# Value projections of two mixers in one set of 512-column products, and where they stand

## The chip, the cores and the metric

The program runs on one core of one Trainium2 chip. The metric is the device time of one execution in microseconds (us). Five engines matter: TensorE (products; its weight loads are listed apart as PEld), VectorE (DVE), ScalarE (ACT), GpSimd (POOL) and SyncE (SP), whose queue issues all DMAs. Each engine runs its own instructions in a fixed order and waits on semaphores for the others.

## What is computed

Two transformer blocks, each of two layers, on one sequence of 512 tokens with 1024 features. The change is in the first block. A layer of it is a gated feed-forward, a stage of four mixers, and another feed-forward. All mixers read one projection of the normalised input `z = rmsnorm(x) @ w_in`:

```python
(aq, ak, av, iq, ik, iw, bq, bk, bv, bg, br, cu, dcq, dckv, dkpe) = split(z)
y_a = dsa_mixer(aq, ak, av, iq, ik, iw, ...)   # attention on the 128 best keys of an index
y_b = gla_mixer(bq, bk, bv, bg, br, ...)       # gated linear attention
y_c = conv_mixer(cu, ...)                      # gate, causal convolution of 31 taps, norm, silu
y_d = mla_mixer(dcq, dckv, dkpe, ...)          # attention on latents, with rotated parts
x = x + concat(y_a, y_b, y_c, y_d) @ w_out
```

`av` and `bv`, the values of mixers A and B, are 256 columns each; they are plain projections of `x`. The values of mixer D come from the 128 latents of `dckv` and have 256 columns too.

## The kernel before

Activations lie with features on the 128 partitions and the 512 tokens in columns; 128 x 512 float32 numbers fill one of the eight PSUM banks. To keep float32 accuracy every operand is split into a high part and a rest (`wh`, `wl` of the weights, `xnh`, `xnl` of the input), and each product is three TensorE instructions (`mm3`, lines 196 to 198: high by high, high by rest, rest by high).

**Weights.** `Model.fill` takes them in the order that `order` lists: a DMA of up to 512 KB into one of three `raw` buffers, a ScalarE copy that rounds to `wh` (line 181), a VectorE subtraction that gives `wl` (line 182). Three pairs of `wh`/`wl` exist. `weights` keeps up to two loads ahead of the one that is asked for.

**The order of work.** The kernel is written in a framework that plans the instructions when the program is built: the order in which the code issues them is a priority, and the planner, with modelled times of its own, puts on each engine's queue the first by priority that it takes to be ready, and a later one where an earlier would wait. The chip then runs each queue in that fixed order, also where the real times are others.

**The mixers' stage** (`Mixers.run`) issues: the misc and latent projections, mixer A's index scores, `d_heads` (mixer D's queries, keys and values; its norms need spread products `sp`, line 592, and rotation products `rot`, line 1052), and `c_prep` (the four `cu` projections of 24 products each; its result is written to DRAM as `hp_d`). Then, interleaved by generators: eight steps of mixer D's attention (`d_attend`); with each, one of sixteen rounds of mixer A's top-k on VectorE (`a_topk`) and three steps of a side chain: `c_conv`, `a_values`, `a_heads`, `c_out`. After that come the rest of the top-k, `b_heads` (projections `bq`, `bk`, each taken from PSUM by VectorE, line 523), `b_values`, `b_gates` (`br0`, `br1`), `a_bias` (tables of mixer A's position bias, loaded into tiles that D's attention frees), and mixer A's attention `a_attend`, whose bias products are line 772, with the rest of mixer B beside it.

**The convolution** takes two halves of 128 channels. For each half it loads taps (line 954) and shifted rows of `hp_d` (line 957, four DMAs) into a tile of tag `gq`, of which there is one, then issues 32 products of 32 rows by 512 columns in plain float32 (line 962; each shows as two records) and a copy from PSUM. Between loads and products stands one `yield`.

**The values.** `values` (line 556 on) makes 128 tokens by 256 columns at a time: 24 products with the tokens' input as weights and 256 columns of `w_v` moving, then a ScalarE eviction (line 565); four blocks for A, four for B. The results of A lie two blocks to a tile in R2 and R3, of B in R0 and R1; `d_heads` uses R0 to R4 before. Projections and values share two PSUM banks (tag `mm`). In `d_heads` the four blocks of D's values (name `uv`) each take a bank of `mm` for 256 columns and an eviction (line 1035).

Of the kernel before, what the change touches and what calls it, by code (L numbers as in the profile page):

```python
# [10 lines left out]
FR = mybir.dt.float32r  # L11
# [3 lines left out]
AF = mybir.ActivationFunctionType  # L15
# [5 lines left out]
KD = D // 128  # L21
# [11 lines left out]
def pack_values(w):  # L33

    return np.ascontiguousarray(w.reshape(2, 4, 128, 256).transpose(0, 2, 1, 3))


def cols(v):
# [23 lines left out]
class Model:  # L62
# [107 lines left out]
    def fill(self, n):  # L170

        nc = self.nc
        while len(self.loaded) < n and self.todo:
            src = self.todo.popleft()
            flat = src if len(src.shape) == 2 else src.rearrange("p a b -> p (a b)") if len(src.shape) == 3 \
                else src.rearrange("p a b c d -> p (a b c d)") if len(src.shape) == 5 else src.rearrange("p a b c -> p (a b c)")
            cols = flat.shape[1]
            raw = self.wp.tile([128, cols], F32, name="raw", tag="raw", bufs=NRAW)
            nc.sync.dma_start(raw, flat)
            h, l = (self.wp.tile([128, cols], FR, name=n, tag=n, bufs=3) for n in ("wh", "wl"))  # L180
            nc.scalar.activation(h, raw, AF.Copy)  # L181
            nc.vector.tensor_tensor(l, raw, h.bitcast(F32), op=ALU.subtract)  # L182
            self.loaded.append((src, (h, l)))
# [161 lines left out]
LEAD = 16  # L345
LOOKAHEAD = 2
NRAW = 3
PARTS = ((0, 8), (8, 7), (15, 7))
HALVES = (slice(0, S // 2), slice(S // 2, S))

# [94 lines left out]
def host_pack_mixers(I, P, vadd):  # L445
    for l in range(2):
        w = I["w_in"][l]
        misc = np.zeros((D, 128), w.dtype)
        for n, c, r in (("ik", 32, 0), ("dkpe", 32, 32), ("iw", 8, 64), ("bg", 16, 96)):
            misc[:, r:r + c] = w[:, IN_OFF[n]:IN_OFF[n] + c]  # L450
        t = [misc]
        for n in IN_TILES[1:]:
            b, j = (n[:-1], int(n[-1])) if n[-1].isdigit() else (n, 0)
            t.append(w[:, IN_OFF[b] + 128 * j:IN_OFF[b] + 128 * (j + 1)])
        P[f"w_in{l}"] = pack_T(np.concatenate(t, axis=1))
        P[f"w_v{l}"] = np.stack([pack_values(w[:, IN_OFF[n]:IN_OFF[n] + 256]) for n in ("av", "bv")])
        uq = I["d_uq"][l].reshape(256, 4, 96)
        uq = np.concatenate([uq[:, :, :64].reshape(256, 256), uq[:, :, 64:].reshape(256, 128)], axis=1)
        P[f"d_uq{l}"] = np.ascontiguousarray(pack_T(uq).transpose(1, 0, 2, 3))
        ukv = I["d_ukv"][l].reshape(128, 4, 128)  # L460
        P[f"d_ukv{l}"] = np.ascontiguousarray(
            np.concatenate([ukv[:, :, :64].reshape(128, 256), ukv[:, :, 64:].reshape(128, 256)], axis=1))
        g = np.zeros((128, 128), np.float32)
        g[96:112] = I["b_gate_up"][l]
        P[f"b_up{l}"] = g

        wo = I["w_out"][l]
        P[f"w_out{l}"] = pack_T(np.concatenate([wo[512:768], wo[768:1024], wo[256:512], wo[0:256]], axis=0))
        two = lambda a: np.tile(a.reshape(1, -1), (2, 1)).reshape(-1, 1)
        vadd(f"a_q_norm{l}", two(I["a_q_norm"][l]))  # L470
        vadd(f"a_k_norm{l}", two(I["a_k_norm"][l]))
        vadd(f"b_gate_bias{l}", cols(I["b_gate_bias"][l]))
        vadd(f"b_out_norm{l}", two(I["b_out_norm"][l]))
        w = I["c_dw_w"][l][:, 0, :]
        taps = np.zeros((2, 4, 32, 4, 8, 32), w.dtype)
        c = np.arange(32)
        for k in range(31):
            taps[:, k % 4, c, :, k // 4, c] = w[k].reshape(2, 4, 32).transpose(2, 0, 1)
        P[f"c_taps{l}"] = taps.reshape(2, 128, 4, 8, 32)
        vadd(f"c_b{l}", cols(I["c_dw_b"][l]))  # L480
        vadd(f"c_norm{l}", cols(I["c_norm"][l]))
        vadd(f"d_qa_norm{l}", cols(I["d_qa_norm"][l]))
        vadd(f"d_kva_norm{l}", cols(I["d_kva_norm"][l]))
        for n in ("d_q_norm", "d_k_norm"):
            a = I[n][l]
            vadd(f"{n}_n{l}", two(a[:64]))
            vadd(f"{n}_p{l}", np.tile(a[64:].reshape(1, -1), (4, 1)).reshape(-1, 1))
    P["rel_bias"] = I["rel_bias"]
    for n, c in constants().items():
        P["c_" + n] = c  # L490


class Phase:
# [61 lines left out]
    def values(self, w, out):  # L555
# [3 lines left out]
        for t in range(4):  # L559
# [4 lines left out]
                M.mm3(o, (M.xn[k][0][:, r], M.xn[k][1][:, r]), (ws[k // 4][0][:, s], ws[k // 4][1][:, s]), k == 0, k == KD - 1)  # L564
            nc.scalar.activation(out(t), o, AF.Copy, scale=self.rn[:, t:t + 1])


    def gather_squares(self, out, tiles):

# [63 lines left out]
class Mixers(Phase):  # L633


    def order(self):

        ap, l = self.ap, self.l
        p = lambda *ns: [ap[f"w_in{l}"][IN_TILES.index(n)] for n in ns]
        v = lambda i: [ap[f"w_v{l}"][i, c] for c in range(2)]  # L640
        return p("misc", "dcq0", "dcq1", "dckv", "iq0", "iq1") + [ap[f"d_uq{l}"], ap[f"d_ukv{l}"]] + \
            p("cu2", "cu0", "cu3", "cu1") + v(0) + p("aq0", "aq1", "ak0", "ak1", "bq", "bk") + v(1) + p("br0", "br1") + \
            [ap[f"w_out{l}"][m, :, 4 * i:4 * i + 4] for i in range(2) for m in range(KD)]

    def proj(self, name):
# [131 lines left out]
                yield  # L777


    def b_values(self):  # L780
        two = [self.z(f"vB{i}", f"R{i}") for i in range(2)]
        self.vB = [two[t // 2][:, 256 * (t % 2):256 * (t % 2) + 256] for t in range(4)]
        self.values(self.ap[f"w_v{self.l}"][1], lambda t: self.vB[t])

    def a_values(self):
        two = [self.z(f"vA{i}", f"R{2 + i}") for i in range(2)]
        self.vA = [two[t // 2][:, 256 * (t % 2):256 * (t % 2) + 256] for t in range(4)]
        self.values(self.ap[f"w_v{self.l}"][0], lambda t: self.vA[t])

    def b_heads(self):  # L790
        self.bq = self.take(self.proj("bq"), "bq", "Q0", scale=32 ** -0.5)
# [210 lines left out]
    def d_heads(self):  # L1002
# [22 lines left out]
        raw = [raw[0], raw[1], raw[3], raw[4], raw[2], kpr]  # L1025
        self.dv = []
        ch, cl = self.ckv[0]
        for t in range(4):
            o = M.psum_mm("uv")[:, :256]
            r = slice(t * 128, (t + 1) * 128)  # L1030
            M.mm3(o, (ch[:, r], cl[:, r]), (ukv[0][:, 256:512], ukv[1][:, 256:512]), True, True)
            if t % 2 == 0:
                dv = self.z(f"dv{t // 2}", f"dv{t // 2}")
            v = dv[:, 256 * (t % 2):256 * (t % 2) + 256]
            nc.scalar.activation(v, o, AF.Copy)
            self.dv.append(v)
        g = M.psum("gD")
        self.gather_squares(g, [(t, [(i, i // 2 * 2)] if i < 4 else [(2 * i - 8, 2 * i - 5), (2 * i - 7, 2 * i - 4)])
                                for i, t in enumerate(raw)])
# [60 lines left out]
    def run(self, last_tile):  # L1100
        with ExitStack() as st:
# [6 lines left out]
            def chain(*fs):  # L1108
                for f in fs:
                    g = f()  # L1110
                    if g is not None:
                        yield from g
                    yield
# [7 lines left out]
            self.d_heads()  # L1121
            self.c_prep()
            topk = self.a_topk()
            side = chain(self.c_conv, self.a_values, self.a_heads, self.c_out)
            for _ in self.d_attend():
                step(topk)
                step(side, n=3)
# [1 line left out]
                for _ in g:  # L1129
                    pass  # L1130
            self.b_heads()
            self.b_values()
            self.b_gates()
            self.a_bias()
            self.yC = [self.split_y(t) for t in self.cacc]
# [802 lines left out]
```

## Time and profile before

| what | before |
|---|---|
| device time, median of 3 runs | 3290.86 us (3290.36 to 3291.94) |
| the profiled execution | 3292.49 us, its span 3290.7 us |
| TensorE busy | 3200.9 us (97%) |
| VectorE busy | 1732.0 us (53%) |
| ScalarE busy | 1319.8 us (40%) |
| mean granted TensorE clock | 0.991 |
| mixers' stage, first layer | about 378 to 700 us |
| mixers' stage, second layer | about 1411 to 1730 us |

A profile is one execution. A record has a start, a duration and, in brackets, the idle time of its engine before it and what ended that. Products overlap in TensorE's pipeline, so the cost of one is read from the distance between starts, not from its duration. The granted clock is the share of full TensorE speed in a stretch; a value between the two levels is a mean over them.

### The profile page before, as it was taken

To read this page: it belongs to the slowest core of one execution; us is meant where nothing else is said; L and a number is where in the kernel's file an instruction comes from. 1 tells how busy PE (TensorE), PEld (TensorE's weight loads), DVE (VectorE), ACT (ScalarE), POOL (GpSimd) and SP (SyncE) were. 2 spreads that over 40 slices of the span, in tenths; PEclk is the share of its full clock that TensorE was granted. 3 is DMA by queue.
4 is the path that set the end of the run, shared out by engine and by line. 5 is a ranking of instruction groups with operands and counts; after the bars stand their busy time and mean duration, and the time that the engine had idled before them with its cause. 6 is when DMAs were issued, how large, how long until landed. Compare 5 with 4: busy or idle time off the path is not lost.

```text
span 3290.7 us, 38872 instructions
## 1 busy us (share of the span) xinstructions
PE 3200.9 (97%) x15174; PEld 2566.7 (78%) x15178; DVE 1732.0 (53%) x2767; ACT 1319.8 (40%) x2041; POOL 187.2 (6%) x184
## 2 busy tenths in 40 slices
PE   8999999999999999999999999998999999989998
PEld 6888856788888888875778888876788887778887
DVE  5443468664433444357774443687554428664433
ACT  4232346743323332243763322355533227643322
POOL 1000100010000000010010000000200011010000
PEclk9999999999999999999999999999999999999999
DMA  4333341033333332343113333322233332323332
GB/s 158 111 97 97 108 128 61 26 107 100 97 94 100 96 96 93 100 126 98 49 62 96 96 93 100 113 79 58 93 96 96 93 100 71 102 71 96 97 95 79
DMA packets 114473, 306.65 MB, mean 93 GB/s; under 512 B 21840, under 2 KB 35056, under 8 KB 114288
## 3 DMA queue, kind: packets, MB, share of 16 engines
q1 hardware_dynamic: 114288, 304.16, 29.9%
q8 instruction: 119, 1.95, 0.2%
q14 instruction: 66, 0.54, 0.0%
HBM read 292.18 MB, written 10.09 MB: 92 GB/s over the span
## 4 chain that ended last, share of the span: by engine, by line
PE 86%; DVE 6%; ACT 4%; DMA 3%; issue 1%; SPq 0%; POOL 0%; DVEq 0%; ACTq 0%; POOLq 0%
PE gu L196 14%; PE gu L197 14%; PE gu L198 14%; PE o L197 8%; PE o L198 8%; PE o L196 8%; DMA conv<-hp_d 1%; PE conv L962 1%; PE wo L197 1%; PE wo L196 1%; PE wo L198 1%; PE lgD L1080 1%; PE v L196 1%; DVE wl L182 0%; PE v L197 0%
## 5 line engine op out<-in xcount | busy, mean ns | idle before, releaser
L181 ACT ACTIVATE wh<-raw 128x1024 fp32r<-128x1024 f32 (+2 forms) x550 | 550.3, 1001 | 1492.9 <-PE gu L197 843.0
L182 DVE TENSOR_TENSOR wl<-raw,wh 128x1024 fp32r<-128x1024 f32 (+2 forms) x550 | 633.0, 1151 | 547.3 <-ACT wh L181 542.7
L196 PE MATMUL o<-hid,wh 128*128 128x512 f32 (+1 forms) x1100 | 419.2, 381 | 0.0
L197 PE MATMUL o<-hid,wh 128*128 128x512 f32 (+1 forms) x1100 | 418.9, 381 | 0.0
L198 PE MATMUL o<-hid,wl 128*128 128x512 f32 (+1 forms) x1100 | 418.5, 380 | 0.0
L315 DVE SCALAR_TENSOR_TENSOR us<-gu,rstd 128x512 f32<-128x512 f32 x132 | 91.2, 691 | 400.7 <-PE gu L198 400.7
L196 PEld LDWEIGHTS o<-hid,wh 128*128 128x128 f32 x1100 | 206.8, 188 | 39.9
L197 PEld LDWEIGHTS o<-hid,wh 128*128 128x128 f32 x1100 | 206.8, 188 | 39.8
L198 PEld LDWEIGHTS o<-hid,wl 128*128 128x128 f32 x1100 | 206.8, 188 | 39.1
L313 DVE SCALAR_TENSOR_TENSOR gs<-gu,rstd 128x512 f32<-128x512 f32 x132 | 91.3, 692 | 259.3 <-PE gu L198 258.5
L272 POOL TENSOR_TENSOR sqacc<-sqacc,sq 128x512 f32<-128x512 f32 x70 | 104.2, 1488 | 369.4 <-ACT sq L267 367.4
L318 ACT ACTIVATE hid<-gs 128x512 fp32r<-128x512 f32 x132 | 83.5, 632 | 93.1 <-DVE gs L316 93.1
L196 PE MATMUL gu<-xn0h,wh 128*128 128x512 f32 x258 | 103.3, 400 | 0.0
L197 PE MATMUL gu<-xn6l,wh 128*128 128x512 f32 x258 | 100.6, 390 | 1.9 <-DVE xn6l L261 1.9
L197 PE MATMUL gu<-xn0l,wh 128*128 128x512 f32 x258 | 100.9, 391 | 0.0
L198 PE MATMUL gu<-xn0h,wl 128*128 128x512 f32 x258 | 100.9, 391 | 0.0
L198 PE MATMUL gu<-xn1h,wl 128*128 128x512 f32 x258 | 100.9, 391 | 0.0
L197 PE MATMUL gu<-xn1l,wh 128*128 128x512 f32 x258 | 100.9, 391 | 0.0
L197 PE MATMUL gu<-xn2l,wh 128*128 128x512 f32 x258 | 100.9, 391 | 0.0
L196 PE MATMUL gu<-xn1h,wh 128*128 128x512 f32 x258 | 100.9, 391 | 0.0
L196 PE MATMUL gu<-xn2h,wh 128*128 128x512 f32 x258 | 100.8, 391 | 0.0
L198 PE MATMUL gu<-xn2h,wl 128*128 128x512 f32 x258 | 100.7, 390 | 0.0
(1386 smaller groups left out, 7069.9 us busy)
## 6 DMA issues: line engine op xcount, KB each, us to landing
raw<-in_ffn_gu SPq DMA_DIRECT2D x176, 512.0 KB
raw<-in_f_gu SPq DMA_DIRECT2D x88, 512.0 KB
raw<-in_ffn_d SPq DMA_DIRECT2D x64, 448.0 KB
raw<-in_w_in SPq DMA_DIRECT2D x36, 512.0 KB
raw<-in_ffn_d SPq DMA_DIRECT2D x32, 512.0 KB
raw<-in_f_d SPq DMA_DIRECT2D x32, 448.0 KB
raw<-in_w_out SPq DMA_DIRECT2D x32, 256.0 KB
raw<-in_f_d SPq DMA_DIRECT2D x16, 512.0 KB
```

The source lines that it names most:

```text
L181: nc.scalar.activation(h, raw, AF.Copy)
L182: nc.vector.tensor_tensor(l, raw, h.bitcast(F32), op=ALU.subtract)
L196: t.matmul(out, lhsT=wh, rhs=xh, start=first, stop=False)
L197: t.matmul(out, lhsT=wh, rhs=xl, start=False, stop=False)
L198: t.matmul(out, lhsT=wl, rhs=xh, start=False, stop=last)
L272: nc.gpsimd.tensor_tensor(self.sq_acc, self.sq_acc, sq, op=ALU.add)
L313: nc.vector.scalar_tensor_tensor(gs, g, -1.0, self.nrstd, op0=ALU.mult, op1=ALU.mult)
L315: nc.vector.scalar_tensor_tensor(us, u, -1.0, self.nrstd, op0=ALU.mult, op1=ALU.mult)
L318: nc.scalar.activation(h, gs, AF.Copy)
L962: nc.tensor.matmul(p[32 * g:32 * g + 32], lhsT=cw[:, g, k], rhs=st[:, g, 4 * k:4 * k + S], start=(k == 0), stop=(k == 7))
L1080: nc.tensor.matmul(lg[:, :C], lhsT=self.dq[h][:, q], rhs=self.dk[h][:, :C], start=True, stop=False)
```

## The change

Both values are made in one set: the weights of `av` and `bv` stand side by side, so that each block of 128 tokens needs 24 products of 512 columns, held in four weight buffers of 512 KB. The set is issued by the side chain between the first convolution half's loads and its products, a block to a step; the second half's products come after mixer A's four projections. `b_values` goes. A fourth pair of weight buffers is made (three `raw` buffers stay), and a scratch area for DMA descriptors is halved. D's values are made two blocks to a bank, with one eviction for both.

```diff
-            h, l = (self.wp.tile([128, cols], FR, name=n, tag=n, bufs=3) for n in ("wh", "wl"))
+            h, l = (self.wp.tile([128, cols], FR, name=n, tag=n, bufs=NW2) for n in ("wh", "wl"))
...
+NW2 = 4
...
+    def values_wide(self, w, out):
+
+        M, nc = self.M, self.nc
+        ws = [M.weights(w[c]) for c in range(4)]
+        for t in range(4):
+            r = slice(t * 128, (t + 1) * 128)
+            o = M.psum_mm("v")
+            for k in range(KD):
+                s = slice((k % 2) * 512, (k % 2) * 512 + 512)
+                M.mm3(o, (M.xn[k][0][:, r], M.xn[k][1][:, r]), (ws[k // 2][0][:, s], ws[k // 2][1][:, s]), k == 0, k == KD - 1)
+            nc.scalar.activation(out(t), o, AF.Copy, scale=self.rn[:, t:t + 1])
+            yield
...
-            p("cu2", "cu0", "cu3", "cu1") + v(0) + p("aq0", "aq1", "ak0", "ak1", "bq", "bk") + v(1) + p("br0", "br1") + \
+            p("cu2", "cu0", "cu3", "cu1") + v + p("aq0", "aq1", "ak0", "ak1", "bq", "bk", "br0", "br1") + \
...
+    def ab_values(self):
+
+        v = [self.z(f"vAB{t}", f"R{t}") for t in range(4)]
+        self.vA = [t[:, :256] for t in v]
+        self.vB = [t[:, 256:] for t in v]
+        yield from self.values_wide(self.ap[f"w_v{self.l}"], lambda t: v[t])
...
-        for t in range(4):
-            o = M.psum_mm("uv")[:, :256]
...
+        for i in range(2):
+            o = M.psum_mm("uv")
+            dv = self.z(f"dv{i}", f"dv{i}")
+            for t in range(2):
+                r = slice((2 * i + t) * 128, (2 * i + t + 1) * 128)
+                c = slice(256 * t, 256 * t + 256)
+                M.mm3(o[:, c], (ch[:, r], cl[:, r]), (ukv[0][:, 256:512], ukv[1][:, 256:512]), True, True)
+                self.dv.append(dv[:, c])
+            nc.scalar.activation(dv, o, AF.Copy)
...
-            side = chain(self.c_conv, self.a_values, self.a_heads, self.c_out)
+            conv = self.c_conv()
+            part = lambda: next(conv)
+            side = chain(part, self.ab_values, part, part, self.a_heads, part, self.c_out)
...
             self.b_heads()
-            self.b_values()
             self.b_gates()
...
-    nc = bacc.Bacc("TRN2", target_bir_lowering=False, num_devices=1, dynamic_dma_scratch_size=2048)
+    nc = bacc.Bacc("TRN2", target_bir_lowering=False, num_devices=1, dynamic_dma_scratch_size=1024)
```

## Rows read from the trace of the kernel before

**Rows 1.** The page, part 1: busy us, share of the span, instructions, by engine.

```profile
PE 3200.9 (97%) x15174; PEld 2566.7 (78%) x15178; DVE 1732.0 (53%) x2767; ACT 1319.8 (40%) x2041; POOL 187.2 (6%) x184
```

**Rows 2.** Stretch, length, busy us (PE, PEld, DVE, ACT, POOL), granted clock, DMA share, GB/s.

```profile
460.00:482.00 22.00, 18.63 (x86) 5.71 (x85) 13.40 (x23) 2.88 (x4) 0.00 (x0) 0.84 0.32 100
482.00:507.00 25.00, 22.16 (x159) 12.72 (x158) 20.18 (x57) 6.10 (x22) 0.20 (x1) 1.00 0.26 79
507.00:565.00 58.00, 58.00 (x289) 40.87 (x287) 52.85 (x132) 38.36 (x72) 2.48 (x4) 1.00 0.17 55
565.00:592.00 27.00, 26.36 (x188) 23.42 (x186) 12.92 (x18) 18.20 (x31) 0.53 (x1) 1.00 0.26 89
592.00:655.00 63.00, 59.33 (x359) 42.01 (x361) 44.76 (x119) 48.30 (x133) 0.00 (x0) 1.00 0.06 17
1494.00:1515.00 21.00, 17.76 (x83) 5.28 (x82) 12.69 (x22) 2.55 (x4) 0.00 (x0) 0.84 0.33 103
```

**Rows 3.** Waits of TensorE, whole kernel: us in total, times, longest us.

```profile
PE conv L962 <- DMA conv<-hp_d: 12.8, 10, 2.8
...
PE gb L196 <- ACT wh L181: 1.4, 3, 0.9
```

**Rows 4.** Timeline of TensorE: start, us, instruction, idle before and its releaser.

```profile
460.17 0.39 PE L198 MATMUL cu<-xn7h,wl 128*128 128x512 f32 x1
...
465.96 1.92 PE L962 MATMUL conv<-conv 128*32 128x512 f32 x2 [2.79 <-DMA conv<-hp_d]
...
478.39 1.12 PE L1052 MATMUL rot<-kpr,c_rot 128*128 128x512 f32 x2
...
480.14 1.06 PE L962 MATMUL conv<-conv 128*32 128x512 f32 x6
...
481.13 0.38 PE L197 MATMUL v<-wl,xn1h 128*128 128x256 f32 x1
```

**Rows 5.** Timeline of TensorE, 490 to 507 us.

```profile
490.38 0.28 PE L196 MATMUL v<-wh,xn6h 128*128 128x256 f32 x1
...
501.36 5.35 PE L962 MATMUL conv<-conv 128*32 128x512 f32 x46
...
506.64 0.39 PE L196 MATMUL v<-wh,xn1h 128*128 128x256 f32 x1
```

**Rows 6.** Timeline of TensorE: first products of sets of 24, 512 and 256 columns.

```profile
454.92 0.40 PE L196 MATMUL cu<-xn0h,wh 128*128 128x512 f32 x1
...
483.86 0.28 PE L196 MATMUL v<-wh,xn0h 128*128 128x256 f32 x1
...
486.74 0.28 PE L196 MATMUL v<-wh,xn0h 128*128 128x256 f32 x1
```

**Rows 7.** Timeline of TensorE: first latent value product, and the product behind the last.

```profile
423.41 0.28 PE L196 MATMUL uv<-wh,sh 128*128 128x256 f32 x1
...
427.67 0.80 PE L196 MATMUL cu<-xn0h,wh 128*128 128x512 f32 x1 [0.47 <-ACT dv L1035]
```

**Rows 8.** Timeline of ScalarE: a 512-column eviction.

```profile
419.85 0.60 ACT L1014 ACTIVATE uq<-uq 128x512 f32<-128x512 f32 x1
```

**Rows 9.** Timeline of VectorE: two waits, and the take of bq.

```profile
472.64 0.75 DVE L1049 SCALAR_TENSOR_TENSOR uq<-uq,vecs,sp 128x512 f32<-128x512 f32 x1 [8.16 <-PE sp L592]
...
509.10 1.23 DVE L182 TENSOR_TENSOR wl<-raw,wh 128x1024 fp32r<-128x1024 f32 x1 [5.55 <-ACT wh L181]
...
565.34 0.68 DVE L523 SCALAR_TENSOR_TENSOR bq<-bq,rstd 128x512 f32<-128x512 f32 x1
```

**Rows 10.** Timeline of SP's DMA queue: loads of the convolution's rows.

```profile
452.93 2.62 SPq L957 DMA_DIRECT2D conv<-hp_d  x4
```

**Rows 11.** Timeline of TensorE: first vB product, first bias product of mixer A's attention.

```profile
566.08 0.39 PE L196 MATMUL v<-wh,xn0h 128*128 128x256 f32 x1 [0.64 <-DVE bq L523]
...
591.85 0.33 PE L772 MATMUL lgA<-toep,ident_r 128*128 128x128 f32 x2
```

**Rows 12.** Groups by line, ScalarE, 2100 to 2420 us: full-size weight splits.

```profile
L181 ACT ACTIVATE wh<-raw 128x1024 fp32r<-128x1024 f32 x26 | 27.4, 1056 | 26.6 <-PE gu L197 19.9 <-PE gu L223 3.1 <-PE o L197 1.3
```

More of the change, by code (lines that the diff above doesn't have):

```diff
@@ L35, in pack_values, with pack_wide @@
     return np.ascontiguousarray(w.reshape(2, 4, 128, 256).transpose(0, 2, 1, 3))
+def pack_wide(w):
+    return np.ascontiguousarray(w.reshape(4, 2, 128, 512).transpose(0, 2, 1, 3))
 def cols(v):
@@ L455, in host_pack_mixers @@
         P[f"w_in{l}"] = pack_T(np.concatenate(t, axis=1))
-        P[f"w_v{l}"] = np.stack([pack_values(w[:, IN_OFF[n]:IN_OFF[n] + 256]) for n in ("av", "bv")])
+        P[f"w_v{l}"] = pack_wide(np.concatenate([w[:, IN_OFF[n]:IN_OFF[n] + 256] for n in ("av", "bv")], axis=1))
         uq = I["d_uq"][l].reshape(256, 4, 96)
@@ L639, in order @@
         p = lambda *ns: [ap[f"w_in{l}"][IN_TILES.index(n)] for n in ns]
-        v = lambda i: [ap[f"w_v{l}"][i, c] for c in range(2)]
+        v = [ap[f"w_v{l}"][c] for c in range(4)]
         return p("misc", "dcq0", "dcq1", "dckv", "iq0", "iq1") + [ap[f"d_uq{l}"], ap[f"d_ukv{l}"]] + \
-            p("cu2", "cu0", "cu3", "cu1") + v(0) + p("aq0", "aq1", "ak0", "ak1", "bq", "bk") + v(1) + p("br0", "br1") + \
+            p("cu2", "cu0", "cu3", "cu1") + v + p("aq0", "aq1", "ak0", "ak1", "bq", "bk", "br0", "br1") + \
             [ap[f"w_out{l}"][m, :, 4 * i:4 * i + 4] for i in range(2) for m in range(KD)]
@@ L777, in a_attend @@
                 yield
[L780 to L788, printed above, removed]
+    def ab_values(self):
[3 more added lines that the diff above has]
+        yield from self.values_wide(self.ap[f"w_v{self.l}"], lambda t: v[t])
     def b_heads(self):
@@ L1027, in d_heads @@
         ch, cl = self.ckv[0]
-        for t in range(4):
-            o = M.psum_mm("uv")[:, :256]
[L1030 to L1036, printed above, removed]
+        for i in range(2):
[7 more added lines that the diff above has]
+            nc.scalar.activation(dv, o, AF.Copy)
         g = M.psum("gD")
```

## The prediction

> **What bounds the kernel now.** First the page's busy times: TensorE works 97% of the span, every other engine 53% or less [rows 1]. Whatever is to be gained must therefore leave TensorE's path: fewer or cheaper products, or its waits. Next the busy time by stretch of the first layer's mixers [rows 2], where one looks at TensorE's busy time together with the granted clock. In 460 to 482 us TensorE is busy 18.63 of 22.00 us and the granted clock is 0.84 (a mean over its two levels, 1.2 and 2.4 GHz: part of this stretch ran at the lower one). In 482 to 507 it is busy 22.16 of 25.00, in 507 to 565 all the time. The second layer repeats it (1494 to 1515: 17.76 of 21.00, again 0.84). Third the waits of TensorE by releaser: the longest sum in the whole kernel is the convolution's products waiting for their loads [rows 3].
>
> Fourth, TensorE's own timeline, read by start times, since a record's busy time hides a slow product. The last product of the preceding projection starts at 460.17, the first undisturbed value product at 481.13 [rows 4]. A product of 512 columns takes 0.228 us at full clock (23 steps from 454.92 to 460.17, [rows 4, 6]), so this stretch is 20.7 us long. What stands in it: 64 convolution records, which cost 0.115 us each where nothing disturbs them (46 records from 501.36 to 506.64, [rows 5]), 7.4 us; the spread and rotation products of `d_heads`, 3.5 us by their starts, of which the last group, 478.39 to 480.14, is shown; four value products at 0.12, 0.5 us. That is 11.3, so **9.4 us is lost** to missing data and to the low clock behind it. The same sum for the second channel half: 490.50 to 506.64 is 16.1 us, with 64 records (7.4), 12 small attention records and 8 value products (2.6 us by starts): **6.2 us lost**. In a list-scheduled program the products that could fill these holes exist, but the order puts the convolution's products before them.
>
> **The change part by part** (per layer; there are two).
>
> *Values between the convolution's loads and products.* The loads of the convolution's rows are issued from 452.93 on [rows 10], and a product still waits for them at 465.96 [rows 4], so they take 13 us and a little more. After the change 96 products of 512 columns, 96 x 0.228 = 21.9 us, stand ahead of the first half's products, which then come after 480; and the four `aq`/`ak` projections (also 96 products, 21.9 us) stand between the second half's loads and its products, more than the 13 us too. Both waits are covered: 9.4 + 6.2 = 15.6 us off TensorE. If the cover fails, the same amounts come back.
>
> *One 512-column set instead of two of 256.* 24 products of 256 columns take 2.88 us (483.86 to 486.74), 0.120 each [rows 6]; two of them 0.240 against 0.228. 96 pairs x 0.012 = 1.2 us saved. The trace says more than the Trainium skill here: "TensorE: Matmul & The Clock Gate", section "Back-to-back issue gap", gives N/2.4 + 2.5 ns, 109 and 216 ns, so by the page a pair saves only 2.5 ns, an estimated 0.2 us in all. By the page the total below would be 2 us less; the rows decide.
>
> *`vB` leaves the tail.* Today the B values stand after the attention of mixer D, between TensorE's wait for the take of `bq` (its end is the end of the DVE row at 565.34, [rows 9]) and the `br` projections: 96 x 0.12 = 11.5 us of the 25.8 us to the first bias product of the next attention at 591.85 [rows 11]. Moving them costs nothing by itself, but they were cover: `br0` now waits for `bq`'s take in their place (banks: two), and behind `br0` stand `br1` and the whole attention of mixer A. VectorE's side of that: it is busy 13.40 + 20.18 + 52.85 = 86.4 us between 460 and 565 [rows 2], and gets 2.4 us more (two weight splits of 1.23 us come earlier). Of its idle time 8.16 us is the wait for the spread product, which itself stood behind the stalled convolution, and 5.55 us a split that waited for ScalarE, which waited for weight buffers [rows 9]. The first goes with the stall. TensorE will reach `br0` at about 564.2 - 15.6 + 10.4 (longer values) - 1.0 = 558; VectorE, with 88.8 us of work from 460, at its present density without these two gaps (86.4 of 91.3 us) is there at 554, with the second gap at 559.4, with both at 568. The new wait is 0 to 10 us; I take 1.5, near the case that keeps one gap. Even if VectorE gained nothing, the stage after it would begin 11.5 us earlier, since `vB` no longer follows. The bias loads go into the tiles that mixer D's attention frees, and move with that attention.
>
> *Where the new products may wait.* All four weight pairs are held from the first to the last value block, so the next projection's split waits on ScalarE until the last block has passed its second k; 18 products (4.1 us) remain, and the split takes 1.06 + 1.23 [rows 9, 12]. Both banks for products are full after two blocks (11 us), and their evictions go to R0 and R1, which are free only when `d_heads` has read them, about 10 us after the spread product, so near 474: a hole of 0 to 3 us, in which the convolution's products can run if their data is there. The last two weight pairs arrive within the first block. Together 0 to 4 us, I take 1.5.
>
> *The next stage is denser.* ScalarE works 18.20 of 27 us in 565 to 592 and 48.30 of 63 after that [rows 2]; the tail shrinks by 11 to 15 us and loses four evictions and two splits. 0 to 3 us may come back as waits of TensorE; I take 0.8.
>
> *Latent values two to a bank.* Four rounds from 423.41 to 427.67 [rows 7], 1.07 us each: 0.36 of products, 0.71 of eviction and its two hand-overs. Two rounds of 0.72 + 0.71, and some 0.2 for twice the columns (a 512-column eviction is 0.60 in all, [rows 8]), make 3.3: 1.0 us saved, all of it on TensorE's path.
>
> *Fourth weight pair, smaller scratch.* TensorE hardly waits for splits (the longest sum is 1.4 us in the whole kernel, [rows 3]); 0 to 2 us of gain, I take 0. The halved scratch changes no instruction and no transfer that the page lists: 0.
>
> **Sum.** Per layer 15.6 + 1.2 + 1.0 = 17.8, less 1.5 + 1.5 + 0.8 = 14.0; twice, 28 us. The profiled execution took 3292.5 (span 3290.7 and 1.8 around it), so 3264.5 for such a one; the median of the three runs shown is 1.6 lower, 3290.9, which gives **3263 us**.
>
> **The rivals.** *(a) One wait stays.* The planner fills TensorE by its own modelled times; if it again puts one half's products where the rows have not landed, 12.4 us (second half) or 18.8 us (first half) are not gained: 3275 or 3282. For it: in the present order it did place them too early, by up to 8 us. Against: 21.9 us of ready products now come first. *(b) The change doesn't do what it says*: both halves' products stay ahead of the values, 31.2 us not gained, charges paid: 3294, no measurable difference. *(c) More:* no charge at all, 2 x 17.8 = 36, 3255, and up to 2 us more from the fourth pair. *(d) Slower:* the fourth pair lets every split come one weight earlier on ScalarE and VectorE. In the even layer's attention, where both feed TensorE, 26 full-size splits of 1.06 us stand on ScalarE [rows 12], with a 1.23 us half each on VectorE. If all went ahead of softmax work that TensorE waits for, that is 59 us: 3322. It cancels the gain from 12 of the 26 on, and makes the kernel measurably slower from 15 on. Against it: ScalarE is idle for 26.6 us before these very splits.
>
> **How the numbers follow.** Forecast (3258 to 3270) 0.58; (c) 0.12; (a) 0.14; (b) 0.09; (d) 0.07. The range 3253 to 3282 holds the forecast, (a) and nearly all of (c): the upper end is (a)'s larger price, about what all upper charges together (17 a layer, unlikely at once) would also give. About 0.2% (6.6 us) is what a measurement of this kernel can tell from no change. Faster: 0.58 + 0.12 + 0.14 = 0.84; same 0.09; slower 0.07.
>
> **What would show it.** Right: no wait of the convolution's products for `hp_d` above 1 us; granted clock 1.00 from 455 to 560; spread products within 5 us of the last `cu` product; the first `v` block beginning right behind `cu`; 0.228 us per value product; about 16 us fewer between the last `cu` product and the first bias product in each layer. Wrong: a wait of `br` for `bq` above 5 us, a second stretch with a granted clock below 1, or a stage 592 to 655 that got longer by more than 3 us. The forecast fails as a whole if the time outside the two mixers moves by more than a few us.

## The result, and the profile of the changed kernel

Four executions of the changed kernel take 3264.95 us in the median (3262.42 to 3265.75), beside 3291.4 us for the kernel before (3290.36 to 3291.97): 26.5 us less, ratio 0.9919 (95% interval 0.9901 to 0.9936). The prediction said 3263 in 3253 to 3282. The profiled execution has a span of 3264.0 us (3290.7 before). The page's busy times (name, busy us, share of the span, instructions), to be laid beside [rows 1]:

```profile
PE 3183.2 (98%) x14982; PEld 2553.4 (78%) x14986; DVE 1733.9 (53%) x2767; ACT 1309.3 (40%) x2025; POOL 193.5 (6%) x184
```

TensorE is still the bound, with 17.7 us less work in its records. Busy time by stretch (columns as in [rows 2]):

```profile
458.00:480.00 22.00, 22.00 (x106) 15.39 (x105) 20.90 (x41) 5.81 (x9) 0.00 (x0) 1.00 0.33 98
480.00:505.00 25.00, 25.00 (x142) 15.18 (x141) 22.92 (x63) 13.40 (x35) 0.00 (x0) 1.00 0.36 117
505.00:562.00 57.00, 57.00 (x323) 35.92 (x322) 47.53 (x118) 34.84 (x68) 2.53 (x4) 1.00 0.17 52
562.00:573.00 11.00, 11.00 (x50) 9.11 (x49) 5.17 (x8) 4.61 (x10) 0.00 (x0) 1.00 0.30 97
573.00:585.00 12.00, 9.12 (x54) 6.50 (x53) 7.25 (x20) 10.13 (x22) 0.53 (x1) 1.00 0.07 22
585.00:600.00 15.00, 15.00 (x73) 11.76 (x72) 9.49 (x28) 12.46 (x39) 0.00 (x0) 0.89 0.06 20
1477.00:1498.00 21.00, 21.00 (x99) 14.53 (x98) 20.49 (x40) 5.48 (x7) 0.00 (x0) 1.00 0.32 99
```

From the last `cu` product (458.38) to 573, TensorE has no idle time and the granted clock is 1.00, where [rows 2] showed 18.63 of 22.00 us at 0.84 and 22.16 of 25.00. Behind it is something new: 573 to 585, the first 12 us of mixer A's attention, has TensorE busy for 9.12 us, and then the clock falls to 0.89. Of TensorE's waits (columns as in [rows 3]) the first line is now the longest sum of the kernel, the second is new; the convolution's wait for `hp_d`, 12.8 us before, is gone from the list:

```profile
PE ms L1268 <- ACT sq L1248: 9.4, 6, 2.9
...
PE bd L834 <- DVE bpd L831: 2.8, 2, 1.4
```

And TensorE's timeline (start, us, instruction, idle before and its releaser):

```profile
458.38 0.39 PE L203 MATMUL cu<-xn7h,wl 128*128 128x512 f32 x1
458.60 0.40 PE L201 MATMUL v<-wh,xn0h 128*128 128x512 f32 x1
...
465.41 0.40 PE L611 MATMUL sp<-rs,spread 128*128 128x512 f32 x1
...
472.76 0.64 PE L978 MATMUL conv<-conv 128*32 128x512 f32 x4
...
574.04 1.08 PE L815 MATMUL pre<-misc,bup 128*128 128x512 f32 x2
```

The values start one step behind `cu`, the first spread product comes 7 us later, and the convolution's products find their rows at 472.76. Of the new hole, the chain of waits (start, us, what; it is followed back from the last instruction) shows what TensorE stood behind:

```profile
573.32 0.70 DVE br L529
...
574.70 1.28 ACT L625
...
578.43 1.28 ACT L821
579.73 0.72 ACT gate_e L821
...
580.63 1.28 ACT L625
...
582.93 1.12 DVE bsum L824
584.05 0.60 DVE bpd L831
584.69 1.06 PE bd L834 x8
```

This is mixer B's gate chain, from `pre` to `bd`: the product `pre` (574.04), activations (`gate_e`), a scan (`bsum`), and the products `bd` of `bpd`; steps of mixer A's softmax (L625) stand between its own on ScalarE. The lines without a tile are table loads of ScalarE, 1.28 us each: two for the softmax, one for `gate_e`. Of the 2.9 us that TensorE waits here, 1.4 are `bd`'s wait for `bpd`; the rest are two waits of 0.7 us for mixer A's own steps. It ends 11.5 us behind the first bias product of mixer A (573.19), while before `bd` stood 0.8 us behind that product (592.62 and 591.85). The three loads are 3.8 of the 10.7 us from `pre` (574.04) to `bd`. The Trainium skill, "ScalarE: Activation LUTs", section "Table sets: the hidden batching unit", tells to group activations by table set, which this chain and the softmax beside it do not; its price of about 2.7 us for a switch does not hold here: a load takes 1.28 us in the rows, and ScalarE's next record starts 0.02 us behind its end (579.73).

All comparisons below rest on one table. It gives differences between starts in TensorE's timeline: from the first `uq` to the last `cu` product, from there to the first bias product, from there to the first `gu` product of the next feed-forward; first and second layer, us. The rightmost column is the ratio of the time to that of the kernel before, run in the same series.

```
                                uq to cu     cu to bias      bias to gu     ratio (95% interval)
before                         43.4  43.5   131.7  131.8    98.7   98.8
changed                        39.4  39.4   114.8  114.8   104.8  106.4    0.9919 (0.9901-0.9936)
e1  latent alone               41.4  41.4   126.4  127.0    98.7   98.7    0.9960 (0.9947-0.9972)
e2  four pairs alone           40.3  40.5   129.4  128.8    98.7   98.7    0.9980 (0.9971-0.9989)
e3  changed, place undone      39.4  39.4   133.1  133.9   103.4  104.8    1.0028 (1.0016-1.0039)
e4  place alone                43.5  43.3   116.6  116.6    98.7   99.8    0.9910 (0.9896-0.9923)
e5  all but wide               39.4  39.4   119.4  119.5    98.7   99.6    0.9918 (0.9905-0.9932)
e6  changed, chain + bd early  39.4  39.4   122.0  120.4    97.6   97.6    0.9915 (0.9902-0.9929)
e7  e6, one weight fewer       39.4  39.4   120.4  118.8    97.5   97.5    0.9912 (0.9899-0.9926)
e8  place + latent             41.3  41.6   125.1  124.8    98.7   98.8    0.9954 (0.9942-0.9967)
e9  changed, bd, then chain    39.5  39.4   117.0  117.0   101.0  101.0    0.9910 (0.9894-0.9927)
e10 e9, one weight fewer       39.4  39.4   117.0  117.0   102.3  102.3    0.9917 (0.9903-0.9932)
e11 changed, chain early       39.4  39.4   115.9  115.7    99.2   99.2    0.9891 (0.9876-0.9905)
e12 changed, again             39.4  39.4   115.0  114.8   104.7  104.7    0.9919 (0.9905-0.9934)
```

So the change is +4.0 (uq to cu), +16.9 (cu to bias), and -6.0 and -7.6 (bias to gu) a layer: 14.9 and 13.5 us. Of the 16.9 gained and of the 6.0 and 7.6 lost, 0.9 us is only `pre`, which stood ahead of the first bias product and now stands behind it. The first feed-forward costs 2.2 us more (first `misc` product at 380.71, before 378.55). What lies behind the second layer's mixers is the same: 1566.7 us before, 1566.0 after, from that last `gu` start to the end of the span.

### The profile page after: what moved, and what is told of

It reads as the page before. It is cut to its first block, busy times and chain, and to the rows that moved or that the text cites. A ratio compares the mean times of both kernels' runs of the same rounds, so it can differ in the third digit from the quotient of the medians.

```text
span 3264.0 us, 38476 instructions
## 1 busy us (share of the span) xinstructions
PE 3183.2 (98%) x14982; PEld 2553.4 (78%) x14986; DVE 1733.9 (53%) x2767; ACT 1309.3 (40%) x2025; POOL 193.5 (6%) x184
## 4 chain that ended last, share of the span: by engine, by line
PE 88%; DVE 7%; ACT 3%; issue 1%; POOL 0%; DMA 0%; SPq 0%; DVEq 0%; ACTq 0%; POOLq 0%
PE gu L202 14%; PE gu L201 14%; PE gu L203 14%; PE o L202 8%; PE o L201 8%; PE o L203 8%; PE conv L978 1%; PE wo L201 1%; PE wo L203 1%; PE wo L202 1%; DVE wl L187 1%; ACT gAqb L864 1%; PE v L201 1%; PE v L202 1%; DVE pn L1296 1%
```

## The experiments

### Which part of the change gives the gain

The theory: the place gives it, since two loads are then covered. Rivals: the width, the values' leaving the tail, or the small parts. Three runs add one part to the kernel before, and one takes the place out of the changed kernel.

**Latent values alone (e1).** The edit is the hunk of `d_heads` in the change, in the kernel before.

> The kernel before with one part of the change: the latent values two to a bank. The prediction's own term is 1.0 us a layer, 2 us in all: 3289.4 beside 3291.4. The trace of the changed kernel says more: from the first uq product to the last cu product 39.42 us against 43.39 in the first layer and 4.1 us less in the second, so 8 us in all, 3283.4. If the 4.0 us came from another part of the change (the fourth weight pair, the first products of cu finding their weights), this run shows 3289 to 3290.

Measured: 3277.88 us, beside 3291.67 for the kernel before in the same series; 13.8 us, more than either figure. The stretch from `uq` to `cu` gained 2.1 us, not 4.0 and not 1.0; the rest (about 5 us a layer) came behind it: its wait for `hp_d` fell from 12.8 to 8.9 us over the kernel, with other orders of the same products.

**Four pairs alone (e2).**

```diff
-            h, l = (self.wp.tile([128, cols], FR, name=n, tag=n, bufs=3) for n in ("wh", "wl"))
+            h, l = (self.wp.tile([128, cols], FR, name=n, tag=n, bufs=NW2) for n in ("wh", "wl"))
...
+NW2 = 4
...
-    nc = bacc.Bacc("TRN2", target_bir_lowering=False, num_devices=1, dynamic_dma_scratch_size=2048)
+    nc = bacc.Bacc("TRN2", target_bir_lowering=False, num_devices=1, dynamic_dma_scratch_size=1024)
```

> The kernel before with one part of the change: four weight pairs and the halved scratch. Theory: only the start changes, because two weight splits come ahead of the work that the first norm waits for, so the first misc product starts 2.2 us later, and all else stays: 3293.6 beside 3291.4. Prediction's term: 0, 3291.4. Rival (d): splits come ahead of softmax work in the even layer, 3300 or more. A fourth possibility is that earlier splits save TensorE waits later, up to 2 us: 3289.

Measured: 3285.53, 0.2% faster. None of the four figures has it; the fourth comes nearest, but is too small, and its reason is not the one that the trace shows. `uq` to `cu` gains 3.1 us a layer, and the stretch behind it 2.3 and 3.0, for which these runs show no cause. The run does not part the fourth pair from the halved scratch. How the first part comes, ScalarE's timeline shows: first the kernel before, then this one.

```profile
422.44 0.59 ACT L1022 ACTIVATE uk<-uk 128x512 f32<-128x512 f32 x1
...
427.23 0.38 ACT L1035 ACTIVATE dv<-uv 128x256 f32<-128x256 f32 x1 [0.71 <-PE uv L198]
...
429.96 0.59 ACT L1022 ACTIVATE uk<-uk 128x512 f32<-128x512 f32 x1
```

```profile
423.40 0.59 ACT L1023 ACTIVATE uk<-uk 128x512 f32<-128x512 f32 x1
424.57 0.60 ACT L1023 ACTIVATE uk<-uk 128x512 f32<-128x512 f32 x1 [0.58 <-PE uk L198]
425.06 0.38 ACT L1036 ACTIVATE dv<-uv 128x256 f32<-128x256 f32 x1
```

The projections and these products share two banks. Before, the eviction of the second `uk` bank was queued behind all four evictions of `uv` and came at 429.96; until then one bank was held, and the `uv` rounds followed each other through the other one, each waiting for its eviction ([rows 7] show the last of these waits). With four pairs the planner puts that eviction at 424.57, ahead of them. Why it orders them otherwise is not settled by these runs.

**The changed kernel with the place undone (e3).**

```diff
-            conv = self.c_conv()
-            part = lambda: next(conv)
-            side = chain(part, self.ab_values, part, part, self.a_heads, part, self.c_out)
+            side = chain(self.c_conv, self.ab_values, self.a_heads, self.c_out)
```

> The changed kernel with the place undone: wide values, latent values two to a bank and four pairs, but the convolution's products issued right behind its loads again. If the place gives the gain: the convolution's products wait for hp_d again (9 us or more in the first half of each layer, clock below 1 there), and the values have left the tail, so mixer B's gate chain is still uncovered; from 3291.4 that is less 8 (latents), less 2.4 (width), plus 2.2 (start), plus 13.6 (6.0 and 7.6 given back in the two stages behind): 3297, slower than before. If the width or the values' leaving the tail gives the gain: near 3265, no wait for hp_d above 1 us.

Measured: 3301.32, 0.28% slower than the kernel before: without the place the rest of the change is a loss. The convolution waits again, for longer than before, and from 485 to 500 us the clock is 0.77:

```profile
PE conv L978 <- DMA conv<-hp_d: 19.1, 13, 2.6
```

```profile
458.00:485.00 27.00, 20.21 (x92) 6.88 (x91) 17.70 (x35) 4.79 (x6) 0.00 (x0) 0.94 0.28 92
485.00:500.00 15.00, 12.28 (x72) 3.20 (x70) 5.30 (x13) 0.86 (x5) 0.00 (x0) 0.77 0.26 80
```

**The place alone (e4).** In the kernel before, three pairs, 256-column values, B values in the tail:

```diff
-            side = chain(self.c_conv, self.a_values, self.a_heads, self.c_out)
+            conv = self.c_conv()
+            part = lambda: next(conv)
+            side = chain(part, self.a_values, part, part, self.a_heads, part, self.c_out)
```

> The kernel before with the place alone: the separate 256-column A values stand between the convolution's loads and its products, the B values stay in the tail, three pairs, latents as before. By the place theory the second half's wait goes whole (6.2 us, the four aq/ak projections are ahead of it), and the first half's falls from 9.4 to about 4 us, since the planner puts one convolution product behind 13 value products of 0.12 us, 1.6 us after cu, and the rows are not there before 5.8 us after it: 11.6 us a layer, 3268. The stage behind the bias products should keep its 98.7 us, since the B values still cover mixer B's gate chain. If 512 columns are needed as cover, the first half gains nothing: 3279 (2 x 6.2). If the values' leaving the tail were the gain, 3291.

Measured: 3262.09 (3260.02 to 3263.17), as fast as the whole change, from an edit of three lines. The wait for `hp_d` is gone, and the stage behind the bias products keeps its 98.7 and 99.8. From `cu` to the bias product 15.1 and 15.2 us are gained. The expected 4 us of wait in the first half did not come:

```profile
459.57 0.39 PE L198 MATMUL cu<-xn7h,wl 128*128 128x512 f32 x1
...
461.44 1.04 PE L962 MATMUL conv<-conv 128*32 128x512 f32 x2
...
469.74 0.64 PE L962 MATMUL conv<-conv 128*32 128x512 f32 x4
```

One convolution product, 1.9 us behind `cu`, found its rows (the loads were issued at 452.36); the others come at 469.74, behind values and spread products. So 512 columns were not needed as cover.

### Where the stage behind the bias products went

**All but the wide values (e5).** This is e4 with the edits of e1 and e2.

> The changed kernel without the wide values: the A values alone stand in 256-column products between the convolution's loads and its products, the B values are back in the tail; four weight pairs and the latent values two to a bank are kept. If the B values were what covered mixer B's gate chain, the stage from the first bias product to the next feed-forward is 98.7 us again in both layers (104.8 and 106.4 in the changed kernel); the stretch from the last cu product to the first bias product is about 116.6 us as in the run with the place alone (114.8 in the changed kernel), and the stretch from uq to cu stays 39.4: per layer 6.8 less and 1.8 more, 10 us in all, 3255 beside 3265 for the changed kernel. If that stage is longer because ScalarE and VectorE meet a denser attention, it stays above 103 us and the time is 3263 to 3268.

Measured: 3262.28. The theory's point holds: with the B values back in the tail, the stage is 98.7 and 99.6 again. The sum does not (3255 was expected): the stretch before it is 119.4, not 116.6. Three waits of 0.5 to 1.2 us appear (`conv` for `hp_d` 0.54, `v` for the eviction of `vA` 1.16, `lgD` for `dk` 1.16), and TensorE is busy 7.68 of the 10 us from 475 to 485. e4 has the same work ahead of the convolution with a later `cu`, the changed kernel the same early `cu` with twice the work, and neither has these waits; that the two together bring them is argued, not tested. The wide values therefore win 4.6 us a layer there and lose 5 to 7 in the stage behind; together a small loss that does not show in the time.

**Gate chain and `bd` early (e6).**

```diff
             self.b_heads()
+            for f in (self.b_prep, self.b_diag):
+                for _ in f():
+                    pass
             self.b_gates()
-            side = chain(self.b_prep, self.b_diag, self.b_levels, self.b_out)
+            side = chain(self.b_levels, self.b_out)
```

> The changed kernel with one thing more: mixer B's gate chain (the pre product, its activations and scan, and the bd products) issued between the bq/bk projections and the br projections, instead of behind br; the planner puts pre ahead of br and bd between the br products. Theory: the chain then runs under br, the first level product comes within 14 us of the first bias product (22.6 in the changed kernel, 13.9 before), and the stage from the first bias product to the feed-forward falls from 104.8 and 106.4 to 98 to 100 us: 10 to 13 us off, 3252 to 3255, less up to 3 if bd waits inside br. Rival (denser ScalarE and VectorE): the stage keeps 103 us or more, 3262 or more.

Measured: 3261.17. The stage fell as the theory had it, to 97.6, but the stretch before grew by 7.1 and 5.6 us; the sum of both (219.5 and 217.9) is nearly that of the changed kernel (219.6 and 221.2). What was lost stands between the `br` products; TensorE's and VectorE's timelines, then the stretches:

```profile
571.51 0.68 PE L834 MATMUL bd<-c_headsel,bpd 128*128 128x4 f32 x3 [1.85 <-DVE bpd L831]
```

```profile
568.92 0.69 DVE L822 TENSOR_TENSOR la<-la,gate_e 128x512 f32<-128x512 f32 x1 [4.19 <-ACT gate_e L821]
...
570.79 0.67 DVE L831 TENSOR_TENSOR bpd<-bq,bk 128x512 f32<-128x512 f32 x1
```

```profile
570.00:574.00 4.00, 2.49 (x10) 2.40 (x11) 2.76 (x6) 2.36 (x4) 0.52 (x1) 0.71 0.00 0
574.00:578.00 4.00, 4.00 (x11) 3.03 (x11) 1.33 (x4) 4.00 (x15) 0.00 (x0) 0.50 0.23 66
```

`bpd` needs only `bq` and `bk`, but VectorE runs in order, and `bpd` stood behind `la` and the scan, which waited 4.19 us for ScalarE's part of the chain. `bd` waited for it 1.85 us amid `br`; TensorE was busy 2.49 of 4.00 us, and from 572 to 578 the granted clock was 0.50, the 1.2 GHz level, where the `br` products took 0.43 instead of 0.23 us. Not all of the 7.1 us is the price of that: `pre` and `bd` now stand in this stretch, which alone costs 2.2 us (e9). The hole and the clock cost about 5 us in the first layer and 3.4 in the second, where the same wait of 1.85 us was followed by a clock of 0.78.

**The same, and one weight fewer ahead at the start (e7).**

```diff
-        self.todo, self.loaded = deque(srcs), deque()
+        self.todo, self.loaded, self.ahead = deque(srcs), deque(), 1
...
-        self.fill(1 + LOOKAHEAD)
+        self.fill(1 + self.ahead)
...
                 ready = self.dense_first([gu(i) for i in range(2)], "gu", (slice(0, S),))
+                self.ahead = LOOKAHEAD
```

> The same as the run with the early gate chain, and the first feed-forward asks for one weight ahead less until its first two products are done, so that at the start no fourth split comes ahead of the first norm's work. Theory: the first misc product comes at 378.6 us (378.55 in the kernel before, 380.71 in the changed one) and the time is 2 us below the run with the early gate chain, near 3251. Rival: the 2.2 us at the start are scatter between executions (the kernels with three pairs started misc at 377.81, 378.55 and 379.57), and the time is the same within 1 us.

Measured: 3260.06, against 3261.17: not told apart. `misc` started at 379.05.

**`bd` first, then the chain (e9).** `b_diag` is cut in two: `bpd` (in tile `Q3`) and `bd` first, then `b_prep`, then `br`; the `gA` part stays behind.

```diff
             self.b_heads()
+            self.b_first()
+            for _ in self.b_prep():
+                pass
             self.b_gates()
-            side = chain(self.b_prep, self.b_diag, self.b_levels, self.b_out)
+            side = chain(self.b_diag, self.b_levels, self.b_out)
```

> The run with the early gate chain, with its bd products issued ahead of that chain instead of behind it (bpd in a tile of its own, so that VectorE takes bpd right behind the take of bk and not behind the chain's ScalarE steps). Theory: in that run TensorE lost 6 to 7 us inside br, because bd waited 1.85 us for bpd behind the chain and the granted clock then fell to 0.50. Here bd finds its data, br takes 11 to 12 us at clock 1.00, the stretch from the last cu product to the first bias product is 115 to 116 us, and the stage behind it 97.6 to 100: 5 to 7 us a layer below the changed kernel, 3251 to 3255. Rival: the stage is only 97.6 because the attention began late; with an earlier attention it goes back to 103 or more, and the sum of both stretches stays at the 217.9 to 219.5 of the run with the early chain: 3260.

Measured: 3261.83; the rival had it. `bd` found its data (564.22) and the clock is 1.00 from 560 to 610, but the sum of both stretches is 218.0. Now mixer A's softmax is late, on ScalarE (first TensorE, then ScalarE):

```profile
581.38 0.30 PE L633 MATMUL lgA<-c_ident,P 128*128 128x128 f32 x1 [2.35 <-DVE nm L626]
```

```profile
576.87 1.56 ACT L847 ACTIVATE gAqb<-c_ident,bd 128x128 f32<-128x128 f32 x5
...
578.97 1.28 ACT L625 ACT_TABLE_LOAD   x1
580.26 0.37 ACT L625 ACTIVATE P<-lgA,nm 128x128 f32<-128x128 f32 x1
```

With `bd` early the `gA` activations are ready early, and stand ahead of the first exponential.

**The same, one weight fewer ahead at the start (e10).** e9 with the edit of e7.

> The same with one weight fewer asked ahead at the start. In the pair of runs with and without it the first misc product came 1.75 us earlier (379.05 against 380.80). Theory: the same again, 1.5 to 2 us below the run before it in this list, 3249 to 3253, with misc at 379. Rival (scatter): no difference in time.

Measured: 3264.98 (3261.5 to 3267.48) against 3261.83 (3261.46 to 3263.62): no gain. `misc` came at 380.36 against 380.86. The stage is 1.3 us longer than in e9 in both layers. TensorE waits 2.37 us at the same product as in e9 (2.35), but here the clock is 0.68 from 580 to 584, and 1.00 there.

**The chain alone early, `bd` left behind (e11).**

```diff
             self.b_heads()
+            for _ in self.b_prep():
+                pass
             self.b_gates()
-            side = chain(self.b_prep, self.b_diag, self.b_levels, self.b_out)
+            side = chain(self.b_diag, self.b_levels, self.b_out)
```

> The changed kernel with the pre product and the gate chain ahead of br, but the bd products left behind it (the planner puts them after the first bias products). Theory: br is not interrupted (11 us, clock 1.00), the chain's ScalarE and VectorE steps run under br, and the level products start some 5 us sooner than in the changed kernel; what stays is bd and the 16 gA activations (4.8 us on ScalarE) ahead of the level products: 3 to 5 us a layer, 3255 to 3259. If the chain's place is worth nothing and only bd counts: 3264.

Measured: 3255.62 (3254.0 to 3258.43), ratio 0.9891, the fastest of all and 8.7 us below the changed kernel in the same series. The stage is 99.2 in both layers, for 1.0 us more in the stretch before, which is `pre` itself. The three stretches to compare with 562 to 600 above:

```profile
562.00:574.00 12.00, 12.00 (x53) 9.56 (x52) 6.99 (x11) 10.60 (x16) 0.53 (x1) 1.00 0.22 67
574.00:586.00 12.00, 11.57 (x71) 9.21 (x70) 7.88 (x27) 10.78 (x35) 0.00 (x0) 1.00 0.13 44
586.00:600.00 14.00, 13.19 (x78) 9.63 (x77) 9.93 (x28) 13.62 (x39) 0.00 (x0) 1.00 0.08 20
```

Under `br` ScalarE is now busy 10.60 of 12 us (4.61 of 11 in the changed kernel), and TensorE 11.57 of the next 12 us (9.12 of 12), at clock 1.00 throughout.

**The changed kernel again (e12).** No edit.

> The changed kernel itself beside the three others on the same chip: 3265, misc at 380.7 if the start's 2.2 us belong to the program, nearer 378.5 if they are scatter; first bias product to feed-forward 104.8 and 106.4 again.

Measured: 3264.29 (3264.02 to 3268.9), `misc` at 381.00, stage 104.7 twice; of the 106.4 in the first profile 1.7 us are scatter (the clock was 0.59 there from 1604 to 1612, here 0.79).

### The place with the latent values (e8)

e4 with the edit of e1.

> The kernel before with the place and the latent values two to a bank, three weight pairs. From the run with the place alone (3262.1): the stretch from uq to cu shrinks by the 2.1 us a layer that the latent values alone gave: 3258. If the fourth pair is needed for that stretch's other 1.9 us a layer (it lets ScalarE evict the second uk bank before the dv evictions), this run keeps 41.4 us there, and the run with everything but the wide values shows 39.4. If the latent values gained only because the convolution's wait shrank behind them, nothing is gained here: 3262.

Measured: 3274.26, 12 us slower than the place alone (14 by the ratios, since the two ran in different series), outside all three expectations. The 2.1 us from `uq` to `cu` are there, but the stretch behind is 8.2 to 8.5 us longer. TensorE, then ScalarE, then SP's queue:

```profile
506.17 0.69 PE L614 MATMUL lgD<-c_ident,P 128*128 128x128 f32 x2 [5.79 <-ACT P L609]
```

```profile
503.19 1.06 ACT L181 ACTIVATE wh<-raw 128x1024 fp32r<-128x1024 f32 x1 [10.67 <-DMA raw<-in_w_in]
...
504.67 0.46 ACT L606 ACTIVATE P<-lgD,nm 128x256 f32<-128x256 f32 x1
```

```profile
461.92 0.33 SPq L179 DMA_DIRECT2D raw<-in_w_in  x1
...
483.95 0.33 SPq L954 DMA_DIRECT2D conv<-in_c_taps  x1
...
487.65 3.18 SPq L179 DMA_DIRECT2D raw<-in_w_in  x2
```

and SP's queue with the place alone:

```profile
461.44 0.34 SPq L179 DMA_DIRECT2D raw<-in_w_in  x1
...
465.62 0.33 SPq L179 DMA_DIRECT2D raw<-in_w_in  x1
...
482.99 0.33 SPq L179 DMA_DIRECT2D raw<-in_w_in  x1
485.11 0.33 SPq L954 DMA_DIRECT2D conv<-in_c_taps  x1
```

The second half's convolution loads wait for the tile that the first half's products free (SP waits 9.7 us for it; their first one is issued at 483.95). With the place alone two weight loads were issued ahead of them, at 465.62 and 482.99; here none, since the planner's order is another, and the next weights were asked for at 487.65. ScalarE, in order, waited 10.67 us for them in front of the softmax's exponential, and TensorE 5.79 us for that. Most of the rest of the 8 us is the clock behind this wait (0.81 from 508 to 516) and a wait of 0.9 us before a B value. An edit that gained 13.8 us by itself cost 12 beside another one: each edit makes the planner write a new order on all queues.

## Why the prediction was right

The total was right by 2 us, and the largest term by half a microsecond. That the total came so near is in part luck: the other terms were off by 1 to 7 us a layer, with both signs, and cancelled.

**The convolution's two waits, 15.6 us: right.** The place alone gained 15.1 and 15.2 us in that stretch, with no other part of the change in it, and undoing it in the changed kernel lost 18.3 and 19.1 there (e3). The signs named for it came, but for one: no wait for `hp_d`, clock 1.00 from 458 to 573, values right behind `cu`; the spread product was later than said (7 us, not 5).

**One 512-column set, 1.2 us: right in price, wrong in balance.** 30 value products start from 458.60 to the spread product at 465.41, 0.227 us each, as forecast. The Trainium skill ("TensorE: Matmul & The Clock Gate", section "Back-to-back issue gap") gives the 0.216 us that the prediction drew on for an isolated product, and about 0.131 for one in a stream; these rows show neither. But the set is only to be had with the B values out of the tail, and that cost 6 us a layer elsewhere (e5).

**Latent values, 1.0, and the fourth pair, 0: mis-sized, 4.0 us together.** The price of the two rounds was right: in e1 they take 3.2 us where the step said 3.3. What the step lacked is what ran at the lower clock behind the slow rounds (the first `cu` product takes 0.80 us in [rows 7]; e1 gained 2.1, not 1.0), and that the rounds were serial for another reason, a bank held by a late eviction of `uk`; that row was in ScalarE's timeline and was not read. The fourth pair's zero rested on TensorE's waits for splits; its gain in this stretch lies in the order of evictions.

**`br`'s wait for `bq` (1.5) and the values' own waits (1.5): not there.** From 458 to 573 TensorE has no idle time at all. So the stretch from `cu` to the bias product gained 16.9 us (0.9 of it the moved `pre`) where the terms gave 13.8 (15.6 + 1.2 - 3.0); these 3.1 us and the 3.0 of the latent part are what the next two items took away again.

**The next stage, 0.8 us: the step that failed; 6.0 and 5.9 to 7.6 us measured.** Of the B values it said "they were cover: `br0` now waits for `bq`'s take in their place", and asked for nothing else that they covered. They covered mixer B's gate chain. The kernel before, TensorE's and VectorE's timelines:

```profile
564.42 1.02 PE L799 MATMUL pre<-misc,bup 128*128 128x512 f32 x2
```

```profile
577.48 0.67 DVE L815 TENSOR_TENSOR bpd<-bq,bk 128x512 f32<-128x512 f32 x1
```

`pre` stood ahead of the first B value (566.08, [rows 11]), the chain ran under 22 us of B value and `br` products, and `bpd` was taken 14 us ahead of the first bias product (591.85, [rows 11]). In the changed kernel the planner's order has `br` first and `pre` behind it (574.04). The 6.0 us of the first layer are 0.9 us of `pre` itself, 2.9 us of waits up to `bd`, and most of the rest the clock behind them (0.79 from 585 to 593). The bound named in the prediction, 0 to 3 us, came from ScalarE's busy share alone, not from the chain. e5 (B values back: 98.7) and e11 (chain early: 99.2) show the cause from both sides; e6 and e9 show that density is the next limit, once `bd` comes early too. Two signs named as "wrong" did come: this stage longer by over 3 us, and a second stretch with a clock below 1 (0.89 from 585 to 600).

**The start, 0: about 2 us lost.** Without the edit of e7, the eight profiles with four pairs have `misc` at 379.5 to 381.0 (mean 380.6), the four with three at 377.8 to 379.6 (mean 378.7). In VectorE's order a fourth weight split stands ahead of three casts there, and TensorE's wait for the first norm's `sq` is 4.1 us instead of 2.0. Asking for one weight less did not mend it measurably.

**The rivals.** None came as described. (d), the even layer's splits ahead of softmax, did not happen: what lies behind the first block takes the same time, as shown above. (b) is e3's kernel: its price there, 3301, shows that the charges of the change without its gain are larger than the 3294 that the rival gave. One sum of the prediction does not come out: all upper charges together (17 a layer) would give 3289, not the 3282 that it sets as the upper end of its range.

## What to carry to other kernels

Put ready products between a load and its first use before anything else is made wider or denser: here a reordering of three lines gave the whole gain. Before moving work out of a place, list every chain that runs under it on the other engines, from its first to its last product, and move the start of that chain too (8.7 us here), but only as much of it as does not get in front of the next stage's first step. In a program that a planner orders, measure parts together as well as alone: e1 and e4 gained 14 and 30 us, both together 15.

## What the runs showed of the hardware

A wait of 1.85 us amid `br` (e6) cost more than itself: the clock stood at 0.50 from 572 to 578, and the stretch took 4.9 us more than in e9, which has the same products in it without that wait. The length of the wait alone does not tell: behind the 2.35 us of e9 the clock stayed at 1.00, behind 2.37 us at the same product in e10 it fell to 0.68. A DMA queue's order reaches TensorE over two engines: a late issue of a weight load on SP (487.65 instead of 465.62) became 10.67 us of ScalarE and 5.79 us of TensorE (e8). A table load of ScalarE takes 1.28 us in every row of all the profiles here.
